# The first two feed-forward blocks of a decoder layer as products of 512 columns

## The chip, the core and the metric

The kernel runs on one core of a Trainium2 chip. The metric is the device time of one execution in microseconds (us); before the change three runs took 1160.81, 1161.96 and 1163.36 us, median 1161.96. One further execution was profiled. A core has a matrix engine (TensorE, PE in the profile; its weight loads are listed as PEld), a vector engine (VectorE, DVE), a scalar engine (ScalarE, ACT), GpSimd (POOL) and a queue that issues transfers (SyncE, SP). A product `lhsT.T @ rhs` on TensorE loads `lhsT` (128 x 128 here) as weights and then streams `rhs`; "a product of 512 columns" streams 512.

## The reference

Two decoder layers on 256 tokens of width 1024. Each has an input projection to 12800 columns that feeds a short convolution, an attention in three head groups and a spatial gating; their gated sum goes through `w_o` and a layer norm; then comes the part that the change touches:

```
h = silu(x @ w_gate) * (x @ w_up)          # w_gate, w_up: 1024 x 2816
x = layer_norm(ALPHA * x + h @ w_down)     # w_down: 2816 x 1024
```

## The kernel before

Everything is float32, and each product of two float32 matrices is done as three products of rounded parts: a matrix is split into a high part h (a rounded copy, made on ScalarE, L179) and a low part l (the rest, made on VectorE, L180), and the kernel sums h·h, h·l and l·h. Activations stay on the chip as such pairs: `xh`, `xl` hold x transposed (features on partitions, 256 tokens). Weights come from memory as panels of 1 MB (class `Panel`, L144), three of them in flight, and are split piece by piece: a piece is 128 partitions x 512 columns, four pieces to a panel, one ScalarE and one VectorE instruction each.

Two helpers issue the products. `feat` (L250) computes a result transposed, 256 features by 256 tokens: a 128 x 128 part of the weights is the stationary side, x streams with 256 columns, and it takes 48 products (L246 to L248) a panel. `toks` (L263) computes a result with tokens on partitions: 128 tokens of x are the stationary side and the weights stream (L266 to L268).

A layer is a list of steps in program order: spatial gating values, attention values, rotary keys and queries, convolution, gating, branch gates, `w_o` (with the norm of each tile of 128 tokens behind it), then the feed-forward blocks of 256 columns, numbered 0 to 10, then `w_down`. Blocks 2 to 10 go through `feat`, a step for the gate and one for the up part. Blocks 0 and 1 are in `ff_first` (L790) and go through `toks`, tile by tile, since tile 0 of x is normed and transposed before tile 1. Their result is in token order and has to be transposed back: `turn_h` (L808) does it on TensorE with the identity, and splits it into `hT`.

The order of instructions on each engine is written out by a pacing routine. Every product adds an estimated cost (`spend`), and each 1300 ns of it gives a `tick` (L209). A tick runs one entry of a list of hooks, among them the transposes of x (`to_features`, L296) and `turn_h`, and splits up to two more weight pieces, depending on how many are ahead of use and whether a hook is pending. So the place of a transpose among the products, and of a split among the work of ScalarE and VectorE, follows from these counts.

Of the kernel before, what the change touches and what calls it, by code (L numbers as in the profile page):

```python
# [14 lines left out]
AF = mybir.ActivationFunctionType  # L15
OP = mybir.AluOpType
# [79 lines left out]
def trunk(ctx: ExitStack, tc: tile.TileContext, a, out):  # L96
    nc = tc.nc
    V = nc.vector
# [11 lines left out]
    def flat(name, dt=F32):  # L110
        live[0] += 1
        assert live[0] <= NS, name
        return sl.tile([128, 512], dt, tag="slot", name=name)

    def slot(name, dt=F32):
        return flat(name, dt).rearrange("p (b s) -> p b s", b=2)

    def free(n=1):
        live[0] -= n
# [4 lines left out]
    def acc():  # L124
        return pa.tile([128, 512], F32, tag="acc", name="acc")

    def trp():
        return pt.tile([128, 512], F32, tag="trp", name="trp")

    con = cp.tile([128, C_N], F32, name="con")  # L130
    ident = con[:, C_ID:C_ID + 128]
# [45 lines left out]
    def split(h, l, src):  # L177

        nc.scalar.activation(h, src, AF.Copy)  # L179
        V.tensor_tensor(l, src, h.bitcast(F32), op=OP.subtract)  # L180
# [15 lines left out]
    def used(n=1):  # L196

        free(2 * n)

    hooks = deque()  # L200
# [8 lines left out]
    def tick():  # L209

        clock[1] += 1
        loaded = False
        while timed and timed[0][0] <= clock[1]:
            timed.pop(0)[1]()
            loaded = True
        if hooks:
            hooks.popleft()()
        clock[2] += PACE if slow else 0
        if clock[2] >= 1:
            clock[2] -= 1  # L220
            slow.popleft()()
            loaded = True
        lead = cnt["made"] - cnt["front"]
        if clock[1] <= cnt["calm"] and lead >= CALM:
            n = 0
        elif lead < LOW:
            n = 2
        elif loaded:
            n = 1 if lead < HIGH else 0
        elif slow:  # L230
            n = 2 if lead < TOP else 1
        else:
            n = 1 + (clock[1] % 2 and not hooks)
        for _ in range(n):
            if cnt["made"] != cnt["hold"] and cnt["split"] < len(panels) and live[0] + 2 + SPARE <= NS:
                piece()

    def spend(ns):
        clock[0] += ns
        if clock[0] >= TICK:  # L240
            clock[0] -= TICK
            tick()
# [7 lines left out]
    def feat(p, rhs):  # L250

        ps = acc()
        for b in range(2):
            for k in range(p.kc):
                mm3(ps[:, b * S:(b + 1) * S], p.at(k, b * 128, 128), *rhs(k), k == 0, k == p.kc - 1)
                if b == 1 and k % 2 == 1:
                    used()
                if b == 0 or k < p.kc - 1:
                    spend(327)
        spend(327)  # L260
        return ps.rearrange("p (b s) -> p b s", b=2)

    def toks(ps, lhs, p, k, c, n, first, last):  # L263

        h, l = p.at(k, c, n)
        nc.tensor.matmul(ps, lhsT=lhs[0], rhs=h, start=first, stop=False)  # L266
        nc.tensor.matmul(ps, lhsT=lhs[0], rhs=l, start=False, stop=False)  # L267
        nc.tensor.matmul(ps, lhsT=lhs[1], rhs=h, start=False, stop=last)  # L268
        if not last:
            spend(1.28 * n)  # L270
# [13 lines left out]
    def xtok(k, t):  # L284
        c = slice(t * 128, (t + 1) * 128)
        return xh[:, k, c], xl[:, k, c]
# [122 lines left out]
    def layer(L, steps):  # L409
# [7 lines left out]
        def half(w, kh, nh):  # L417
            return Panel(w[kh * 512:(kh + 1) * 512, nh * 512:(nh + 1) * 512], 4, 512)
# [89 lines left out]
        c = OFF_V  # L508
# [18 lines left out]
        for g in range(NG):  # L527
            c = OFF_ATT + (3 * g + 2) * GCOL
# [259 lines left out]
        hT = {}  # L788

        def ff_first(P):  # L790

            for j in range(2):
                hT[j] = (slot(f"hh{j}", F32R), slot(f"hl{j}", F32R))
            for t in range(2):
                for j in range(2):
                    ps = acc()
                    for w in range(2):
                        for k in range(8):
                            toks(ps[:, w * 256:(w + 1) * 256], xtok(k, t), P[2 * j + w], k, 0, 256, k == 0, k == 7)
                            if t and k % 2 == 1:  # L800
                                used()
                        if w == 0:
                            spend(328)
                    s = flat("hs")[:, :256]
                    nc.scalar.activation(s, ps[:, :256], AF.Silu)
                    V.tensor_tensor(s, s, ps[:, 256:], op=OP.mult)

                    def turn_h(s=s, t=t, j=j):  # L808
                        pp = trp()
                        for b in range(2):  # L810
                            nc.tensor.transpose(pp[:, b * 128:(b + 1) * 128], s[:, b * 128:(b + 1) * 128], ident)
                        c = (slice(None), slice(None), slice(t * 128, (t + 1) * 128))
                        split(hT[j][0][c], hT[j][1][c], pp[:, :256].rearrange("p (b s) -> p b s", b=2))
                        free()

                    hooks.extend([lambda: None] * 2 + [turn_h])
                    spend(328)

        def ff_gate(j):
            def f(P):  # L820
                ps = feat(P[0], xf)
                s = st["s"] = slot("hs")
                nc.scalar.activation(s, ps, AF.Silu)
            return f

        def ff_up(j):
            def f(P):
                ps = feat(P[0], xf)
                s = st["s"]
                V.tensor_tensor(s, s, ps, op=OP.mult)  # L830
                hT[j] = (slot(f"hh{j}", F32R), slot(f"hl{j}", F32R))
                split(hT[j][0], hT[j][1], s)
                free()
            return f

        ff = [Panel(a[w][L][:, j * 256:(j + 1) * 256], 8, 256) for j in range(11) for w in ("w_gate", "w_up")]
        steps.append((ff[:4], ff_first))
        for j in range(2, 11):
            steps.append(([ff[2 * j]], ff_gate(j)))
            steps.append(([ff[2 * j + 1]], ff_up(j)))  # L840

        dn = {}

# [43 lines left out]
    steps, starts = [], {}  # L887
    for L in range(DEPTH):
        n = len(steps)
        starts[n] = layer(L, steps)  # L890
# [59 lines left out]
```

## Time and profile before

| what | value |
|---|---|
| median of three runs | 1161.96 us |
| profiled execution | 1162.87 us, of which span 1160.8 us |
| PE busy | 1149.6 us (99% of the span) |
| DVE busy | 771.9 us (66%) |
| ACT busy | 619.0 us (53%) |
| granted TensorE clock, mean | 0.998 of full speed |

The busy time of PE says that a product was in flight nearly always, not how far apart products start. Matmuls overlap one another in the trace (a row of 0.28 us can be followed by the next 0.11 us later), so the pace is read from the starts of two rows and the number of products between them.

### The profile page before, as it was taken

What the parts mean: (1) busy time and instruction counts of PE and PEld (TensorE: products, weight loads), DVE (VectorE), ACT (ScalarE), POOL (GpSimd) and SP (SyncE); (2) the same over time, 40 slices, a digit from 0 to 9 for tenths busy, and PEclk for the clock granted to TensorE, in tenths of its full rate; (3) what the DMA queues carried; (4) which work ended last, traced back from release to release, by engine and by line L of the source; (5) the groups of instructions that cost most, each with busy time, mean ns of one, the idle gap of its engine ahead of it and who ended that gap; (6) DMA issues with size and microseconds to landing.
All of it is one profiled execution on the core that took longest, in us unless ns stands there. A gap on an engine that the chain in (4) does not pass through costs nothing.

```text
span 1160.8 us, 21675 instructions
## 1 busy us (share of the span) xinstructions
PE 1149.6 (99%) x8884; PEld 1093.9 (94%) x8884; DVE 771.9 (66%) x1394; ACT 619.0 (53%) x1144; POOL 14.1 (1%) x29
## 2 busy tenths in 40 slices
PE   9999999999999999999999999999999999999997
PEld 7899999999999999998888999999999999999985
DVE  6978778667556776546497677775765568754534
ACT  6655665665445365445175556666654445653530
POOL 0000000000000000000100000000000000000000
PEclk9999999999999999999999999999999999999999
DMA  9688545368557378448357564544666574764630
GB/s 339 211 259 239 169 154 183 112 200 280 165 183 233 105 251 272 162 146 304 131 190 259 171 189 137 182 150 142 211 225 198 175 245 134 253 195 147 215 112 36
DMA packets 180695, 222.41 MB, mean 192 GB/s; under 512 B 5456, under 2 KB 154228, under 8 KB 180596
## 3 DMA queue, kind: packets, MB, share of 16 engines
q1 hardware_dynamic: 178500, 214.66, 56.6%
q0 software_dynamic: 1952, 6.31, 1.7%
q8 instruction: 69, 1.13, 0.4%
q14 instruction: 30, 0.25, 0.1%
q10 hardware_dynamic: 144, 0.07, 0.0%
HBM read 213.67 MB, written 1.05 MB: 185 GB/s over the span
## 4 chain that ended last, share of the span: by engine, by line
PE 94%; DVE 2%; DMA 1%; ACT 1%; issue 1%; SPq 0%; DVEq 0%; ACTq 0%
PE acc L246 21%; PE acc L247 20%; PE acc L248 20%; PE acc L268 9%; PE acc L266 9%; PE acc L267 9%; PE acc L629 1%; PE trp L619 1%; DVE wl L180 1%; DMA raw<-in_w_in 1%; PE acc L708 1%; PE trp L296 1%; PE trp L599 0%; DMA xt<-in_x 0%; DMA sw<-qk 0%
## 5 line engine op out<-in xcount | busy, mean ns | idle before, releaser
L180 DVE TENSOR_TENSOR wl<-raw,wh 128x512 fp32r<-128x512 f32 x776 | 490.5, 686 | 194.7 <-ACT wh L179 188.4
L246 PE MATMUL acc<-xh,wh 128*128 128x256 f32 x1856 | 521.5, 281 | 0.0
L248 PE MATMUL acc<-xh,wl 128*128 128x256 f32 x1856 | 517.4, 279 | 0.4 <-DVE wl L180 0.4
L247 PE MATMUL acc<-xl,wh 128*128 128x256 f32 x1856 | 517.2, 279 | 0.0
L179 ACT ACTIVATE wh<-raw 128x512 fp32r<-128x512 f32 x776 | 429.5, 621 | 66.8 <-DMA raw<-in_w_in 28.3
L248 PEld LDWEIGHTS acc<-xh,wl 128*128 128x128 f32 x1856 | 351.2, 189 | 0.6 <-DVE wl L180 0.6
L246 PEld LDWEIGHTS acc<-xh,wh 128*128 128x128 f32 x1856 | 349.4, 188 | 2.5 <-issue 1.4
L247 PEld LDWEIGHTS acc<-xl,wh 128*128 128x128 f32 x1856 | 349.1, 188 | 0.1
L266 PE MATMUL acc<-wh,xh 128*128 128x512 f32 (+1 forms) x288 | 100.5, 349 | 0.2 <-ACT xh L179 0.2
L267 PE MATMUL acc<-wl,xh 128*128 128x512 f32 (+1 forms) x288 | 98.9, 344 | 0.3 <-DVE wl L180 0.3
L268 PE MATMUL acc<-wh,xl 128*128 128x512 f32 (+1 forms) x288 | 99.1, 344 | 0.0
L266 PE MATMUL acc<-wh,hh 128*128 128x512 f32 x176 | 68.7, 390 | 0.0
L268 PE MATMUL acc<-wh,hl 128*128 128x512 f32 x176 | 68.6, 390 | 0.0
L267 PE MATMUL acc<-wl,hh 128*128 128x512 f32 x176 | 68.6, 390 | 0.0
L267 PEld LDWEIGHTS acc<-wl,xh 128*128 128x128 f32 x288 | 54.9, 191 | 7.1 <-DVE wl L180 1.0
L266 PEld LDWEIGHTS acc<-wh,xh 128*128 128x128 f32 x288 | 54.8, 190 | 6.8 <-ACT xh L179 0.5
L268 PEld LDWEIGHTS acc<-wh,xl 128*128 128x128 f32 x288 | 54.9, 190 | 6.5 <-DVE xl L180 0.4
L179 ACT ACTIVATE hh<-hs 128x512 fp32r<-128x512 f32 x18 | 11.4, 632 | 61.8 <-DVE hs L830 61.8
L316 ACT ACTIVATE sd<-mv,eps 128x1 f32<-128x1 f32 x12 | 3.5, 295 | 74.2 <-DVE mv L313 74.1
L337 DVE SCALAR_TENSOR_TENSOR xt<-xt,acc 128x512 f32<-128x512 f32 x16 | 11.0, 687 | 45.7 <-PE acc L268 45.7
L268 PEld LDWEIGHTS acc<-wh,hl 128*128 128x128 f32 x176 | 33.0, 188 | 6.8
L267 PEld LDWEIGHTS acc<-wl,hh 128*128 128x128 f32 x176 | 33.1, 188 | 6.8
(148 smaller groups left out, 1261.9 us busy)
## 6 DMA issues: line engine op xcount, KB each, us to landing
raw<-in_w_in SPq DMA_DIRECT2D x99, 1024.0 KB, 5.2
raw<-in_w_gate SPq DMA_DIRECT2D x22, 1024.0 KB, 5.6
raw<-in_w_up SPq DMA_DIRECT2D x22, 1024.0 KB, 5.3
raw<-in_w_down SPq DMA_DIRECT2D x22, 1024.0 KB, 4.8
raw<-in_p_a SPq DMA_DIRECT2D x8, 1024.0 KB, 5.2
raw<-in_p_c SPq DMA_DIRECT2D x8, 1024.0 KB, 5.3
raw<-in_w_o SPq DMA_DIRECT2D x8, 1024.0 KB, 5.4
sw<-qk SPq DMA_DIRECT2D x96, 64.0 KB, 2.6
```

What stands on the lines that cost most here:

```text
L179: nc.scalar.activation(h, src, AF.Copy)
L180: V.tensor_tensor(l, src, h.bitcast(F32), op=OP.subtract)
L246: nc.tensor.matmul(o, lhsT=hl[0], rhs=rhs_h, start=first, stop=False)
L247: nc.tensor.matmul(o, lhsT=hl[0], rhs=rhs_l, start=False, stop=False)
L248: nc.tensor.matmul(o, lhsT=hl[1], rhs=rhs_h, start=False, stop=last)
L266: nc.tensor.matmul(ps, lhsT=lhs[0], rhs=h, start=first, stop=False)
L267: nc.tensor.matmul(ps, lhsT=lhs[0], rhs=l, start=False, stop=False)
L268: nc.tensor.matmul(ps, lhsT=lhs[1], rhs=h, start=False, stop=last)
L296: nc.tensor.transpose(ps[:, k * 128:(k + 1) * 128], xt[:, t, (4 * q + k) * 128:(4 * q + k + 1) * 128], ident)
L619: nc.tensor.transpose(ps[:, i * 128:(i + 1) * 128], p[:, i * 128:(i + 1) * 128], ident)
L629: nc.tensor.matmul(o[64 * r:64 * r + 64, t * 128:(t + 1) * 128], lhsT=va[g, kt][:, h * 64:(h + 1) * 64], rhs=state["t", b, t, r][:, i * 12 ...
L708: nc.tensor.matmul(sp[:, (2 * b + n) * 128:(2 * b + n + 1) * 128], lhsT=vv, rhs=st["wsT"][g // 4][:, g % 4, :], start=True, stop=True)
```

## The change

Blocks 0 and 1 are taken together. The weights of both come as half panels of 512 rows by 512 columns (as those of `w_o` do) in place of panels of 1024 rows by 256 columns, two for the gate and two for up. For each tile of 128 tokens the gate of both blocks is one chain of 24 products of 512 columns into one PSUM bank, and up is another into a second bank; before, each block had a bank, with gate and up in its halves, and 48 products of 256 columns. Silu and the multiplication run once a tile on 512 columns, and `turn_h` makes one visit of four transposes a tile where it made two visits of two; its two splits into `hT` stay of 256 columns. Bytes loaded, pieces split and columns streamed stay the same.

```diff
@@ -792,29 +792,29 @@
             for t in range(2):
-                for j in range(2):
-                    ps = acc()
-                    for w in range(2):
-                        for k in range(8):
-                            toks(ps[:, w * 256:(w + 1) * 256], xtok(k, t), P[2 * j + w], k, 0, 256, k == 0, k == 7)
-                            if t and k % 2 == 1:
-                                used()
-                        if w == 0:
-                            spend(328)
-                    s = flat("hs")[:, :256]
-                    nc.scalar.activation(s, ps[:, :256], AF.Silu)
-                    V.tensor_tensor(s, s, ps[:, 256:], op=OP.mult)
-
-                    def turn_h(s=s, t=t, j=j):
-                        pp = trp()
-                        for b in range(2):
-                            nc.tensor.transpose(pp[:, b * 128:(b + 1) * 128], s[:, b * 128:(b + 1) * 128], ident)
-                        c = (slice(None), slice(None), slice(t * 128, (t + 1) * 128))
-                        split(hT[j][0][c], hT[j][1][c], pp[:, :256].rearrange("p (b s) -> p b s", b=2))
-                        free()
-
-                    hooks.extend([lambda: None] * 2 + [turn_h])
-                    spend(328)
+                ps = [acc(), acc()]
+                for w in range(2):
+                    for k in range(8):
+                        toks(ps[w], xtok(k, t), P[2 * w + k // 4], k % 4, 0, 512, k == 0, k == 7)
+                        if t:
+                            used()
+                    if w == 0:
+                        spend(656)
+                s = flat("hs")
+                nc.scalar.activation(s, ps[0], AF.Silu)
+                V.tensor_tensor(s, s, ps[1], op=OP.mult)
+
+                def turn_h(s=s, t=t):
+                    pp = trp()
+                    for b in range(4):
+                        nc.tensor.transpose(pp[:, b * 128:(b + 1) * 128], s[:, b * 128:(b + 1) * 128], ident)
+                    c = (slice(None), slice(None), slice(t * 128, (t + 1) * 128))
+                    for j in range(2):
+                        split(hT[j][0][c], hT[j][1][c], pp[:, j * 256:(j + 1) * 256].rearrange("p (b s) -> p b s", b=2))
+                    free()
+
+                hooks.extend([lambda: None] * 2 + [turn_h])
+                spend(656)
...
-        ff = [Panel(a[w][L][:, j * 256:(j + 1) * 256], 8, 256) for j in range(11) for w in ("w_gate", "w_up")]
-        steps.append((ff[:4], ff_first))
+        ff = {(j, w): Panel(a[w][L][:, j * 256:(j + 1) * 256], 8, 256) for j in range(2, 11) for w in ("w_gate", "w_up")}
+        steps.append(([half(a[w][L], kh, 0) for w in ("w_gate", "w_up") for kh in range(2)], ff_first))
```

The last lines of the diff only fetch the panels of blocks 2 to 10 by name instead of by number.

In the program the change moves instructions at these places. On TensorE, the last visit of `turn_h` in layer 0 stands inside the gate product of block 2 (`acc` is a bank of sums, `trp` a bank for transposes, `hs` silu times up, `con` the identity, `wh` and `wl` the parts of a weight piece; the number behind a name tells one buffer from another). Before it had two transposes:

```order
L246 MATMUL acc_5362<-xh_77,wh_5161 128x256
L247 MATMUL acc_5362<-xl_78,wh_5161 128x256
L248 MATMUL acc_5362<-xh_77,wl_5162 128x256
L811 MATMUL trp_5398<-con_75,hs_5359 128x128 x2
L246 MATMUL acc_5362<-xh_77,wh_5161 128x256
L247 MATMUL acc_5362<-xl_78,wh_5161 128x256
L248 MATMUL acc_5362<-xh_77,wl_5162 128x256
L246 MATMUL acc_5362<-xh_77,wh_5165 128x256
```

The same place now:

```order
L246 MATMUL acc_5262<-xh_77,wh_5122 128x256
L247 MATMUL acc_5262<-xl_78,wh_5122 128x256
L248 MATMUL acc_5262<-xh_77,wl_5123 128x256
L810 MATMUL trp_5300<-con_75,hs_5259 128x128 x4
L246 MATMUL acc_5262<-xh_77,wh_5122 128x256
L247 MATMUL acc_5262<-xl_78,wh_5122 128x256
L248 MATMUL acc_5262<-xh_77,wl_5123 128x256
L246 MATMUL acc_5262<-xh_77,wh_5126 128x256
```

The visit has four transposes instead of two. In layer 0 it stands behind 27 products of `feat`, as before, and 837 follow without a break, as before. In layer 1 it stands behind 21 products where it stood behind 33, so 843 follow where 831 did.

On VectorE, from the end of the norm of tile 1 on, in layer 0 (lines with - are before, with + now; `xl` is the low part of the transposed x of tile 1, `hl` that of `hT`):

```order
 L327 SCALAR_TENSOR_TENSOR xt<-xt,sd,gb 128x512
-L180 TENSOR_TENSOR wl<-raw,wh 128x512 x3
-L806 TENSOR_TENSOR hs<-hs,acc 128x256
-L180 TENSOR_TENSOR wl<-raw,wh 128x512
+L180 TENSOR_TENSOR wl<-raw,wh 128x512 x4
 L180 TENSOR_TENSOR xl<-trp,xh 128x4x128
 L180 TENSOR_TENSOR wl<-raw,wh 128x512 x2
 L180 TENSOR_TENSOR xl<-trp,xh 128x4x128
 L180 TENSOR_TENSOR wl<-raw,wh 128x512 x4
-L806 TENSOR_TENSOR hs<-hs,acc 128x256
-L180 TENSOR_TENSOR wl<-raw,wh 128x512
+L805 TENSOR_TENSOR hs<-hs,acc 128x512
```

The first multiplication of silu and up no longer stands among the weight pieces of tile 0; the one of 512 columns stands behind all of them. Ten pieces of the 16 that tile 0 needs are split ahead of the norm, before as now. On TensorE the transposes of tile 1 of x stand behind 33 and 39 products of 512 columns in layer 0 (30 and 36 in layer 1), where they stood behind 66 and 75 of 256 (57 and 69).

## Rows read from the trace of the kernel before

**Rows 1.** The page's first part: busy us (share of the span) xinstructions.
```profile
PE 1149.6 (99%) x8884; PEld 1093.9 (94%) x8884; DVE 771.9 (66%) x1394; ACT 619.0 (53%) x1144; POOL 14.1 (1%) x29
```
**Rows 2.** Timeline of PE: start us, duration us, line, operation; far-apart products of `feat`.
```profile
278.92 0.28 PE L248 MATMUL acc<-xh,wl 128*128 128x256 f32 x1
...
294.90 0.28 PE L248 MATMUL acc<-xh,wl 128*128 128x256 f32 x1
...
425.04 0.28 PE L247 MATMUL acc<-xl,wh 128*128 128x256 f32 x1
...
514.90 0.28 PE L248 MATMUL acc<-xh,wl 128*128 128x256 f32 x1
```
**Rows 3.** PE in the stretch 1000 to 1090 us: busy (products), clock, DMA share, GB/s.
```profile
1000.00:1090.00 90.00, 90.00 (x766) 1.00 0.60 198
```
**Rows 4.** Timeline of PE at the last visit of `turn_h`, layers 0 and 1.
```profile
418.09 0.28 PE L246 MATMUL acc<-xh,wh 128*128 128x256 f32 x1
...
420.70 0.28 PE L248 MATMUL acc<-xh,wl 128*128 128x256 f32 x1
420.81 0.38 PE L811 MATMUL trp<-con,hs 128*128 128x128 f32 x2
...
421.15 0.28 PE L247 MATMUL acc<-xl,wh 128*128 128x256 f32 x1
...
994.03 0.38 PE L811 MATMUL trp<-con,hs 128*128 128x128 f32 x2
```
**Rows 5.** Timeline of PE at two visits of four transposes (L442) between `feat` products.
```profile
65.19 0.28 PE L248 MATMUL acc<-xh,wl 128*128 128x256 f32 x1
...
67.31 0.28 PE L248 MATMUL acc<-xh,wl 128*128 128x256 f32 x1
67.43 0.60 PE L442 MATMUL trp<-con,ws 128*128 128x128 f32 x4
...
67.99 0.28 PE L247 MATMUL acc<-xl,wh 128*128 128x256 f32 x1
68.11 0.28 PE L248 MATMUL acc<-xh,wl 128*128 128x256 f32 x1
...
73.21 0.28 PE L248 MATMUL acc<-xh,wl 128*128 128x256 f32 x1
73.33 0.60 PE L442 MATMUL trp<-con,ws 128*128 128x128 f32 x4
...
73.88 0.28 PE L247 MATMUL acc<-xl,wh 128*128 128x256 f32 x1
...
79.10 0.28 PE L248 MATMUL acc<-xh,wl 128*128 128x256 f32 x1
```
**Rows 6.** Timeline of PE at a visit of eight transposes (L619) in attention.
```profile
163.50 1.03 PE L619 MATMUL trp<-con,p 128*128 128x128 f32 x8
...
164.61 0.28 PE L248 MATMUL acc<-xh,wl 128*128 128x256 f32 x1
...
168.50 0.28 PE L248 MATMUL acc<-xh,wl 128*128 128x256 f32 x1
```
**Rows 7.** Timeline of PE, products of `toks`: `w_o`, `ff_first`, and layer 1's gating values.
```profile
371.30 0.39 PE L268 MATMUL acc<-wh,ml 128*128 128x512 f32 x1
...
389.00 0.40 PE L268 MATMUL acc<-wh,ml 128*128 128x512 f32 x1
...
393.80 0.28 PE L268 MATMUL acc<-wh,xl 128*128 128x256 f32 x1
...
401.22 0.28 PE L268 MATMUL acc<-wh,xl 128*128 128x256 f32 x1
...
592.12 0.39 PE L268 MATMUL acc<-wh,xl 128*128 128x512 f32 x1
...
608.00 0.40 PE L268 MATMUL acc<-wh,xl 128*128 128x512 f32 x1
```
**Rows 8.** Timeline of VectorE: first weight pieces behind the norm of tile 1, layer 0.
```profile
399.50 1.89 DVE L180 TENSOR_TENSOR wl<-raw,wh 128x512 fp32r<-128x512 f32 x3
```

More of the change, by code (lines that the diff above doesn't have):

```diff
@@ L834, in ff_up @@
             return f
-        ff = [Panel(a[w][L][:, j * 256:(j + 1) * 256], 8, 256) for j in range(11) for w in ("w_gate", "w_up")]
-        steps.append((ff[:4], ff_first))
+        ff = {(j, w): Panel(a[w][L][:, j * 256:(j + 1) * 256], 8, 256) for j in range(2, 11) for w in ("w_gate", "w_up")}
+        steps.append(([half(a[w][L], kh, 0) for w in ("w_gate", "w_up") for kh in range(2)], ff_first))
         for j in range(2, 11):
-            steps.append(([ff[2 * j]], ff_gate(j)))
-            steps.append(([ff[2 * j + 1]], ff_up(j)))
+            steps.append(([ff[j, "w_gate"]], ff_gate(j)))
+            steps.append(([ff[j, "w_up"]], ff_up(j)))
         dn = {}
```

## The prediction

> **What bounds the kernel now.** I read the page's engine shares first: PE is busy for 1149.6 of 1160.8 us [rows 1], so nothing that the other engines save counts by itself; what counts is how far apart products start. That is read from the timeline of PE, by two far rows of a stretch and the number of products from one to the other. The same kind of product, `feat` with 256 columns of x, turns out to run at two paces. From 278.92 to 294.90 us 142 products start [rows 2]: 15.98 us over 141 steps, 113.3 ns each. From 425.04 to 514.90 us, in the feed-forward blocks, 764 start [rows 2]: 89.86 over 763 steps, 117.8 ns each. The stretch from 1000 to 1090 us in layer 1 holds 766 products, a clock of 1.00 and a DMA share of 0.60 [rows 3]; two of the 766 began ahead of it, so 90/764, again 117.8 ns. Both paces come at the full granted clock, and a stretch keeps its pace through hundreds of products, over many weight panels and banks. I call them the close and the wide pace, by the distance of the products.
>
> Where does a pace change? The place that this change touches shows it. In layer 0 the feed-forward blocks from number 2 on begin at the close pace: 24 products from 418.09 to 420.70 [rows 4], 2.61 over 23 steps, 113.5 ns. Then comes the last `turn_h`, two transposes at 420.81 [rows 4], and behind it all 837 remaining products of the stretch are at the wide pace; in layer 1 the visit at 994.03 [rows 4] does the same, and 831 wide ones follow. So the visit decides between the two paces until the next interruption. What differs inside I can't see; I take it as how a product and the weight load beside it lie against each other.
>
> **The change part by part.**
>
> *Products of 512 columns.* A layer loses 192 products of 256 columns and gains 96 of 512. Before: 64 products from 393.80 to 401.22 [rows 7], 7.42/63 = 117.8 ns, so 192 x 117.8 = 22.62 us. The new kind, x as weights and 512 columns streaming, stands in layer 1's gating values: 70 products from 592.12 to 608.00 [rows 7], 15.88/69 = 230.1 ns, so 96 x 230.1 = 22.09 us. Gain 0.53 us a layer, 1.06 in both. From below, `w_o` with its 79 products from 371.30 to 389.00 [rows 7] has 17.70/78 = 226.9 ns, which would give 0.84 a layer, 1.68 in all; from above, two of the old products take 235.6 ns, a gain of nothing. I take 230.1, since there too x is the stationary side.
>
> The Trainium skill, "TensorE: Matmul & The Clock Gate", section "Back-to-back issue gap", gives N/2.4 + 2.5 ns for an isolated product at the full clock: an estimate by it is 2.5 ns saved for each pair, 0.24 us a layer. The rows here stand 9 to 14 ns above that formula, so it gives half of the term above.
>
> *The visits of* `turn_h`. A visit of two: from 420.70 to 421.15 [rows 4] is 0.45 us where two close steps take 0.227, so 0.22 us. A visit of four: from 67.31 to 67.99 [rows 5] is 0.68 where two wide steps take 0.236, so 0.44 us. Eight visits of two cost 1.8 us, four of four 1.8 us: nothing changes.
>
> *The pace behind the last visit.* This is the large term, and the trace has no visit of four at just this place. Its nearest rows are two visits of four transposes (L442) with the same operands, the identity streaming and a 512-column slot as weights. The first interrupts a wide stretch (19 products from 65.19 to 67.31, 2.12/18 = 117.8 ns) that follows on products of `toks` with 512 columns; behind it 46 products from 68.11 to 73.21 take 5.10/45 = 113.3 ns. The second, at 73.33, interrupts that close stretch, and behind it 47 products from 73.88 to 79.10 take 5.22/46 = 113.5 ns [rows 5]. So both visits of four were followed by the close pace, whichever pace they met. The changed kernel copies the first case closely: `feat` follows on 512-column products, and in layer 1 the visit stands behind 21 products, as the one at 67.43 does. So I take the close pace: 837 + 831 = 1668 products at 4.45 ns less are 7.42 us. Against it, `feat` now follows on 512-column products and may begin wide, as at 65.19: 27 + 21 products ahead of the visit at 4.45 ns more, 0.21 us. The term is 7.2 us; its other end is zero (both layers at the wide pace as now, where I also take the 0.21 as lost, 0.2 us below nothing).
>
> *Hidden parts.* Silu and the multiplication run once on 512 columns instead of twice on 256; VectorE and ScalarE are busy 66% and 53% [rows 1], and nothing on PE needs `hT` until `w_down`. The cover that matters is the weight supply of tile 0: it needs 16 pieces within 48 products, ten of them split ahead of the norm. VectorE starts the next three at 399.50 and takes 1.89 us for them [rows 8], the first done at about 400.1. Tile 0 begins two steps of 0.118 ahead of 393.80 [rows 7], at 393.57. The eleventh piece is wanted behind 30 products, at 393.57 + 30 x 0.230 = 400.5, its low part one product later, 400.7. The margin is some 0.6 us, where it was about as much; behind it the change takes one multiplication out of the row of pieces. The transposes of tile 1 of x come at 393.57 + 33 x 0.230 = 401.2, behind the norm that ended when VectorE turned to pieces at 399.50 [rows 8]. If this cover goes, PE waits by what VectorE is late, some tenths of a us. The new panels have rows of 2 KB for 1 KB in the same 1 MB; no load is waited for there, so nothing is booked.
>
> *Sum.* 1.06 + 0 + 7.2 = 8.3 us. The profiled execution took 1162.87 us (span 1160.8 and 2.1 around), which gives 1154.6; the median of the runs is 0.9 lower, 1161.96, so 1153.7 us.
>
> **The rivals.**
>
> *A, the forecast.* Both last visits, of four now, are followed by the close pace: 1153.7, with 1153.0 if 512-column products run as in `w_o`, and 1154.8 if they gain nothing. About 0.7 either way for what a median of three leaves open: 1152.3 to 1155.4.
>
> *B, one layer only.* The two layers reach their visit behind 27 and 21 products, so they can end in different paces: 1161.96 - 1.06 - 3.6 = 1157.3.
>
> *C, the wide pace stays.* The change then does what it says and little comes of it: 1161.96 - 1.06 + 0.2 = 1161.1, at the best 1160.3. For it: a visit is no sure switch. One of eight transposes at 163.50 is followed by 34 products from 164.61 to 168.50 at 3.89/33 = 117.9 ns [rows 6]; and both visits at the very place of the change end wide. Against it: of the 18 visits of four or eight transposes in a row with 256-column `feat` products behind them 16 are followed by the close pace, and the other two have eight.
>
> The Trainium skill, "TensorE: Matmul & The Clock Gate", section "Step-by-step: what each phase is for", says that loading the next weights takes no SBUF read bandwidth from the running product, as each has its own port. By that rule how loads and products lie should not matter, and a visit could not set a pace; the time would be that of C. The rows with two paces at one clock speak against it, so C keeps its chance from the exceptions alone.
>
> *D, slower.* Weight pieces of tile 0 come late. Place: VectorE behind the norm of tile 1, with the low parts of x, 0.7 us each as the pieces' 0.63, in among the last pieces. If a transpose of x slips by more than the 0.6 us of margin, what stands behind it (two pieces, then the other low part) is late, and PE waits up to about 1.9 us a layer. It decides only if the wide pace stays too: 1161.1 + 3.8 = 1164.9. No wait of PE there in the trace now, and one instruction fewer in that row on VectorE, speak against it.
>
> **How the numbers follow.** A 0.60, B 0.10, C 0.25, D 0.05. The prediction is A's 1153.7 us. The range takes in A and B (0.70) and the half of C that lies lower, up to 1161.2: 1152.3 to 1161.2. About 0.2%, 2.3 us, is what a measurement can tell from no change. Faster by more, below 1159.6, are A, B and a little of C: 0.72. Within it is nearly all of C: 0.23. Slower is D: 0.05.
>
> **What would show it.** In the profile of the changed kernel, the starts of `feat` products from the last `turn_h` on: some 794 in a stretch of 90 us if close, 764 if wide, in each layer by itself. The first 27 and 21 products ahead of the visit show whether `feat` begins wide. 96 products of 512 columns should take 22.1 us a layer less their visits. A visit of four should cost 0.44 us. A gap ahead of a product in tile 0 that ends on VectorE would show D. If both stretches are wide, the large term is wrong and what is left is 1 us.

## The result, and the profile after

The changed kernel takes 1155.73 us (median of nine runs, 1153.4 to 1159.5 but for one of 1259 in which the granted clock was 0.85 of full speed), the kernel before 1161.7: a ratio of 0.9945, 95% interval 0.9932 to 0.9957. The forecast was 1153.7 with a range of 1152.3 to 1161.2. The execution that was profiled took 1159.47 us, the longest of the other eight. Its page, first part (busy us, share of the span, instructions):

```profile
span 1157.6 us, 21279 instructions
## 1 busy us (share of the span) xinstructions
PE 1146.5 (99%) x8692; PEld 1081.8 (93%) x8692; DVE 771.9 (67%) x1390; ACT 619.5 (54%) x1140; POOL 14.2 (1%) x29
```

PE is still in use for 99% of the span [rows 1], so the pace of its products is again what to read. PE in three stretches: the feed-forward blocks of layer 0, the rotary products of layer 1 and the feed-forward blocks of layer 1 (columns: the stretch, its length, busy time and the number of products, clock, DMA share, GB/s):

```profile
425.00:505.00 80.00, 80.00 (x709) 1.00 0.64 211
646.00:686.00 40.00, 40.00 (x342) 1.00 0.61 183
1000.00:1075.00 75.00, 75.00 (x639) 1.00 0.57 187
```

The same stretches of the kernel before:

```profile
425.00:505.00 80.00, 80.00 (x681) 1.00 0.67 221
646.00:686.00 40.00, 40.00 (x342) 1.00 0.61 179
1000.00:1075.00 75.00, 75.00 (x639) 1.00 0.61 200
```

A count is the whole finding: 709 products in 80 us is the close pace (113.3 ns, with the two or three that began ahead of the stretch), 681 the wide one (117.8 ns). Layer 0 has changed from wide to close, layer 1 has not. The clock is at its full level in all six rows.

Where the time went is read from the starts of products at the borders of stages, here of the kernel after (first product of `ff_first`, of block 2 and of `w_down`, in layers 0 and 1):

```profile
394.92 0.39 PE L266 MATMUL acc<-wh,xh 128*128 128x512 f32 x1
...
418.39 0.28 PE L246 MATMUL acc<-xh,wh 128*128 128x256 f32 x1
...
516.78 0.39 PE L266 MATMUL acc<-wh,hh 128*128 128x512 f32 x1
...
963.25 0.39 PE L266 MATMUL acc<-wh,xh 128*128 128x512 f32 x1
...
986.71 0.28 PE L246 MATMUL acc<-xh,wh 128*128 128x256 f32 x1
...
1088.85 0.39 PE L266 MATMUL acc<-wh,hh 128*128 128x512 f32 x1
```

| stage | before, us | after, us | difference |
|---|---|---|---|
| up to `ff_first`, layer 0 | 393.57 | 394.92 | +1.35 |
| `ff_first`, layer 0 | 24.17 | 23.47 | -0.70 |
| blocks 2 to 10, layer 0 | 101.88 | 98.39 | -3.49 |
| from there to `ff_first`, layer 1 | 446.48 | 446.47 | 0.0 |
| `ff_first`, layer 1 | 24.17 | 23.46 | -0.71 |
| blocks 2 to 10, layer 1 | 101.85 | 102.14 | +0.29 |
| from there to the end of the span | 68.7 | 68.7 | 0.0 |

The first row is no effect of the change: the two programs are the same there, and in this execution the first loads came later (the first product of `toks` starts at 8.13 us, at 6.86 before); a second trace of the same changed kernel has 393.93 there. Without it the execution would lie near 1158.1 us, by rival B, one layer only, 1157.3. But the median run is over 2 us faster than that, which one trace can't explain. So the experiments ask two things: what sets the pace behind the last visit, and is it the same in each execution?

### The profile page after: what moved, and what is told of

It is laid out like the page before. It is cut to its first block, busy times and chain, and to the rows that moved or that the text cites. A ratio compares the mean times of both kernels' runs of the same rounds, so it can differ in the third digit from the quotient of the medians.

```text
span 1157.6 us, 21279 instructions
## 1 busy us (share of the span) xinstructions
PE 1146.5 (99%) x8692; PEld 1081.8 (93%) x8692; DVE 771.9 (67%) x1390; ACT 619.5 (54%) x1140; POOL 14.2 (1%) x29
## 4 chain that ended last, share of the span: by engine, by line
PE 93%; DVE 3%; DMA 1%; ACT 1%; issue 1%; SPq 0%; DVEq 0%; ACTq 0%
PE acc L246 20%; PE acc L248 20%; PE acc L247 20%; PE acc L266 9%; PE acc L267 9%; PE acc L268 9%; PE acc L629 1%; PE trp L619 1%; DVE wl L180 1%; PE acc L708 1%; DMA raw<-in_w_in 1%; PE trp L296 1%; PE trp L599 0%; DMA xt<-in_x 0%; DMA sw<-qk 0%
## 5 line engine op out<-in xcount | busy, mean ns | idle before, releaser
L266 PE MATMUL acc<-wh,xh 128*128 128x512 f32 x224 | 89.9, 401 | 0.3 <-ACT xh L179 0.3
L267 PE MATMUL acc<-wl,xh 128*128 128x512 f32 x224 | 88.6, 396 | 0.0
L268 PE MATMUL acc<-wh,xl 128*128 128x512 f32 x224 | 88.5, 395 | 0.0
L266 PE MATMUL acc<-wh,hh 128*128 128x512 f32 x176 | 68.7, 390 | 0.0
L266 PEld LDWEIGHTS acc<-wh,xh 128*128 128x128 f32 x224 | 43.1, 192 | 9.3 <-ACT xh L179 0.5
L268 PEld LDWEIGHTS acc<-wh,xl 128*128 128x128 f32 x224 | 42.9, 192 | 9.4 <-DVE xl L180 0.4
L267 PEld LDWEIGHTS acc<-wl,xh 128*128 128x128 f32 x224 | 43.1, 192 | 8.7 <-DVE wl L180 0.2
L266 PEld LDWEIGHTS acc<-wh,hh 128*128 128x128 f32 x176 | 33.0, 188 | 6.8
```

## The experiments

Each verdict is a ratio to the kernel before in the same series, whose medians lay between 1161.7 and 1163.1 us; the single executions stand beside one of it of 1164.27.

**The changed kernel again** (no edit), and later a third time.

> The changed kernel once more, unaltered. Its first profile shows the close pace (113.3 ns) behind the last visit in layer 0 and the wide one (117.8 ns) in layer 1, at 1159.5 us, while eight of its runs lie between 1153.4 and 1159.5. Theory V (the pace behind the visit hangs on how the visit happens to fall, anew in each execution): this profile may show another mix, and its time follows it, about 3.7 us for each of the two stretches; median again near 1155.7. Rival F (each layer's pace is fixed by the program, the spread has another source): again close in layer 0 and wide in layer 1, whatever the time.

Measured: 1155.38 us, ratio 0.9942 (0.9920 to 0.9963). Its profiled execution took 1158.47 us and again had layer 0 close and layer 1 wide.

> The changed kernel once more, for a third trace. Two traces had layer 0 close and layer 1 wide behind the last visit, at 1159.5 and 1158.5 us, while other executions took 1153.4 to 1156.8. If the program fixes the pace (F), layer 1 is wide again; if each execution draws it (V), it may be close, and then the time should be about 1154.5.

Measured: 1155.87 us, and PE of this execution reads

```profile
425.00:505.00 80.00, 80.00 (x708) 1.00 0.65 211
646.00:686.00 40.00, 40.00 (x342) 1.00 0.61 181
1000.00:1075.00 75.00, 75.00 (x664) 1.00 0.60 197
```

664 products in the third stretch in place of 639: layer 1 is close here. One program, two paces at one place in different executions. This run was on another chip than the second one, but the chip doesn't settle it: the two scans below ran on the chip of this run, with the same program up to the last visit of layer 0, and behind that visit layer 0 is wide in the first scan and close in the second. So layer 0 is no sure thing either, close in four of five such traces. F has fallen. The three profiled executions took 1159.5 and 1158.5 us with one layer close and 1155.9 with both, and the runs without a trace between 1153.4 and 1158.3; that most of these had both close is argued from their times, as they have no trace.

**The old products with visits of four.**

```diff
             for t in range(2):
+                both = []
                 for j in range(2):
...
+                    both.append(s)
...
-                        for b in range(2):
-                            nc.tensor.transpose(pp[:, b * 128:(b + 1) * 128], s[:, b * 128:(b + 1) * 128], ident)
+                    for b in range(4):
+                        nc.tensor.transpose(pp[:, b * 128:(b + 1) * 128], both[b // 2][:, b % 2 * 128:(b % 2 + 1) * 128], ident)
```

> The kernel before with its products of 256 columns, but with the two transposes of block 0 and the two of block 1 of a tile in one visit of four (the last one behind 27 and 33 products of block 2, as before, with 837 and 831 behind it). Theory V: the visit alone brings the large part of the gain: at least one of the two stretches at 113.3 ns, 3.7 us for each, so 1154.5 to 1158 us against 1161.7. Rival W (the pace comes from what stands ahead of it, the 512-column products or the half panels): both stretches stay at 117.8 ns, 1161.7 us.

Measured: 1156.06 us, ratio 0.9944 (0.9930 to 0.9959), and

```profile
425.00:505.00 80.00, 80.00 (x708) 1.00 0.65 211
...
1000.00:1075.00 75.00, 75.00 (x664) 1.00 0.62 200
```

Both stretches are close without a single product of 512 columns in these blocks. Grouping the transposes alone brings nearly all of the gain; W has fallen.

**The new products with visits of two.**

```diff
-                    for b in range(4):
-                        nc.tensor.transpose(pp[:, b * 128:(b + 1) * 128], s[:, b * 128:(b + 1) * 128], ident)
+                    for b in range(2):
+                        nc.tensor.transpose(pp[:, b * 128:(b + 1) * 128], s[:, (2 * j + b) * 128:(2 * j + b + 1) * 128], ident)
...
-                hooks.extend([lambda: None] * 2 + [turn_h])
+                hooks.extend([lambda: None] * 2 + [lambda f=turn_h: f(0), lambda f=turn_h: f(1)])
```

> The changed kernel with its 512-column products, but its visits of four taken apart again into two visits of two, one tick (12 products) apart; the last has 825 and 831 products behind it. Theory V: behind visits of two both stretches are at 117.8 ns as in the kernel before; what is left is the products' term, 0.5 us a layer: about 1160.7 us. Rival W: the stretches are at 113.3 ns as far as they were with visits of four, and the time is that of the changed kernel, about 1155.7 us.

Measured: 1155.29 us, ratio 0.9938 (0.9924 to 0.9953). Not what V said: both stretches are close, and the time is the one that W gave, though W can't account for the run before this one.

```profile
425.00:505.00 80.00, 80.00 (x708) 1.00 0.65 211
...
1000.00:1075.00 75.00, 75.00 (x664) 1.00 0.60 197
```

In layer 1 the trace shows the close pace up to the first visit of two (its transposes start at 988.84), the wide one for the 12 products behind it, and the close one behind the second, at 990.47. In layer 0 both visits met the wide pace, and the first left it wide, the second close. So it isn't that two transposes leave the wide pace; what a visit leaves depends on more than its length.

**The last visit out of the way.**

```diff
-                hooks.extend([lambda: None] * 2 + [turn_h])
+                if t == 0:
+                    hooks.extend([lambda: None] * 2 + [turn_h])
+                else:
+                    st["turn"] = turn_h
...
         def ff_up(j):
             def f(P):
+                if j == 10:
+                    st["turn"]()
```

> The changed kernel with the last visit of each layer moved from behind 27 and 21 products to the middle of the last block (816 products ahead of it, 48 behind). Theory V: nothing interrupts the 816 products, so they keep the pace with which they begin behind the 512-column products; where that is close, as in both layers of the changed kernel's first profile, both stretches run at 113.3 ns and the time is about 1153.5 us; where it is wide, 1161. A rival by which layer 1's feed-forward stage is bound to the wide pace by its place (other loads, other buffers) has layer 1 at 117.8 ns again, 1157 us or more.

Measured: 1155.03 us, ratio 0.9931 (0.9914 to 0.9948); 816 products close in both layers (708 and 664 in the two stretches). Nothing in the stage itself forces the wide pace. (The late visit met the close pace in both layers and left the 48 products behind it wide in layer 0, close in layer 1.)

**Which visits leave which pace.** Sixteen visits a layer that do nothing but interrupt, ahead of each panel's first product; `visits` holds eight times 1 and eight times 2 in layer 0, eight times 3 and eight times 4 in layer 1.

```diff
-    def feat(p, rhs):
+    def feat(p, rhs, at=None, n=0):
...
             for k in range(p.kc):
+                if b * p.kc + k == at:
+                    pp = trp()
+                    for i in range(n):
+                        nc.tensor.transpose(pp[:, i * 128:(i + 1) * 128], xt[:, 0, i * 128:(i + 1) * 128], ident)
```

> The changed kernel with 16 further visits in each layer's blocks 3 to 10, each of transposes of x that nobody reads, ahead of a panel's first product: in layer 0 eight visits of one transpose, then eight of two; in layer 1 eight of three, then eight of four. Each is followed by 48 products, whose starts tell the pace. From the runs so far: two transposes met the close pace three times and left the wide one each time; they met the wide one three times and left it wide once and close twice. Theory P (a visit shifts how products and weight loads lie against each other by its length, and the pace that it leaves follows from its length and the pace it meets): for each number of transposes the same pace met leads to the same pace left nearly always; two turn close into wide and come back at the next or the one after it. Rival R (each visit draws the pace afresh): for each number both paces follow without order. Time: 160 transposes at 0.11 us more, and half the blocks at either pace.

Measured: 1165.11 us in one execution (the edit adds 80 transposes, not the 160 of the expectation). Timeline of PE, the second transpose of each of the eight visits of two in layer 0 (start us, duration, line, operation):

```profile
475.45 0.27 PE L258 MATMUL trp<-con,xt 128*128 128x128 f32 x1
...
481.33 0.27 PE L258 MATMUL trp<-con,xt 128*128 128x128 f32 x1
...
487.02 0.27 PE L258 MATMUL trp<-con,xt 128*128 128x128 f32 x1
...
492.71 0.27 PE L258 MATMUL trp<-con,xt 128*128 128x128 f32 x1
...
498.59 0.27 PE L258 MATMUL trp<-con,xt 128*128 128x128 f32 x1
...
504.28 0.27 PE L258 MATMUL trp<-con,xt 128*128 128x128 f32 x1
...
509.97 0.27 PE L258 MATMUL trp<-con,xt 128*128 128x128 f32 x1
...
515.85 0.27 PE L258 MATMUL trp<-con,xt 128*128 128x128 f32 x1
```

From one visit to the next, each time 48 products and two transposes: 5.88, 5.69, 5.69, 5.88, 5.69, 5.69, 5.88 us. Wide, close, close, wide, close, close, wide: an order of three, no draw.

> As the run before it, with each visit behind the panel's first 21 products instead of ahead of them. Theory P: the place doesn't matter, the same pace met and number of transposes lead to the same pace left. A rival by which the place in the panel (which part of x and of the weights is read around the visit) decides has other sequences here.

Measured: 1167.1 us. With the visits at another place in the panel the order of three is the same: behind the visits of two come close, close, wide, close, close, wide, close, close. Taking both runs, 16 visits for each number:

| transposes in the visit | close pace behind it |
|---|---|
| 1 | 3 of 16 |
| 2 | 11 of 16 |
| 3 | 15 of 16 |
| 4 | 15 of 16 |

Of the visits of three and of four it is only the first of a row that missed. The pace that a visit leaves is ordered by its length, but the pace that it meets isn't all that counts: of two visits of two that meet the close pace one goes on close and the next turns wide. It looks like a hidden position, which a visit of two moves through three places, and which differs from execution to execution where a row begins.

**One more visit in the old kernel.** The kernel before, with four transposes added that nobody reads.

```diff
         def ff_up(j):
             def f(P):
+                if j == 2:
+                    pp = trp()
+                    for i in range(4):
+                        nc.tensor.transpose(pp[:, i * 128:(i + 1) * 128], xt[:, 0, i * 128:(i + 1) * 128], ident)
```

> The kernel before, unaltered but for one further visit of four transposes of x that nobody reads, ahead of block 2's up panel in each layer (21 and 15 products behind the last turn_h, 816 ahead of the next break). It adds 0.44 us of work a layer and removes none. In all traces so far a visit of four that met the wide pace left the close one, 9 of 9. Theory P: both stretches run at 113.3 ns, 2 x 816 x 4.45 ns = 7.3 us less, 0.9 us more for the visits, so 6.4 us faster than the kernel before without it (about 1155.5 to 1156.5 by the runs so far). Rival N (the paces are a by-product of other things in the stage, such as when loads or splits fall): 0.9 us slower than before.

Measured: 1157.49 us, ratio 0.9953 (0.9941 to 0.9966). Timeline of PE around the added visit in layer 0, and PE in the two stretches:

```profile
424.59 0.28 PE L248 MATMUL acc<-xh,wl 128*128 128x256 f32 x1
424.71 0.60 PE L831 MATMUL trp<-con,xt 128*128 128x128 f32 x4
425.06 0.37 PE L246 MATMUL acc<-xh,wh 128*128 128x256 f32 x1
```

```profile
425.00:505.00 80.00, 80.00 (x708) 1.00 0.69 224
1000.00:1075.00 75.00, 75.00 (x664) 1.00 0.62 201
```

With eight instructions more and none less the kernel is 5.3 us faster: 681 and 639 products have become 708 and 664. This is the plainest proof that the pace, and no work that the change saves, is the large term. It gained 1.1 us less than the 6.4 expected. The trace shows where: blocks 2 to 10 take 98.70 and 98.67 us in the two layers for 101.88 and 101.85, which is 6.36 us less, as expected, but the stage up to `ff_first` of layer 0, which the edit doesn't touch, takes 394.77 us for 393.57.

**Both visits side by side, meant to make sure of it.**

```diff
+            visits = []
...
-                hooks.extend([lambda: None] * 2 + [turn_h])
+                visits.append(turn_h)
+                if t:
+                    hooks.extend([lambda: None] * 2 + visits)
```

> The changed kernel with tile 0's visit of four held back to stand in block 2's gate and up products too, 12 products behind that of tile 1's place in the order, so that two visits of four follow each other there and no work is added. Theory P: where the first leaves the wide pace the second turns it close, so both layers are close in every execution: median about 1154.3, and none of the executions near 1158 that the changed kernel has (its fast executions lay between 1153.4 and 1159.5). Rival: the spread of the changed kernel has nothing to do with layer 1's pace and is the same here.

Measured: 1162.2 us, ratio 0.9992 (0.9982 to 1.0001): no gain is left that can be told from nothing. A miss, and the most useful one.

```profile
425.00:505.00 80.00, 80.00 (x682) 1.00 0.63 206
1000.00:1075.00 75.00, 75.00 (x639) 1.00 0.60 195
```

Both layers are wide behind the second visit, in this kernel and in the next, four stretches of four. Visits of four 48 products apart kept the close pace in all but the first of a row; 12 products apart they end in the wide one. The products of 512 columns are all there and still save 1.2 us by the stages of this trace, but the large term is gone. Four stretches in two executions are no rule: two of the twelve runs of this kernel, of 1158.97 and 1159.57 us, are some 3 us faster than its median. One close layer is worth 3.7 us, so they may be such cases; they have no trace.

**The rotary products too.** As before, and the transposes of layer 1's spatial weights are held back into the stretch of rotary products, which was wide in all but one trace.

```diff
+            if not first:
+                hooks.extend([lambda: None] * 22)
             for f in st["later"]:
                 hooks.extend([lambda: None] * 3 + [f])
```

> As the run before it, and in layer 1 the two visits of four that transpose the spatial weights (and the one of the filter taps) are held back by 22 ticks, from the attention values into the rotary products, whose 456 products run at the wide pace in eight of nine traces. Theory P: from the second of these visits on some 400 products run at 113.3 instead of 117.8 ns, 1.7 to 2.0 us less than the run before it, about 1152.5. A rival: holding hooks back slows the splitting of weight pieces and PE waits for pieces, no gain or a loss.

Measured: 1160.01 us, ratio 0.9980 (0.9971 to 0.9989), 2.2 us below the run before it, which shares the wide feed-forward stretches. The rotary stretch now holds

```profile
646.00:686.00 40.00, 40.00 (x353) 1.00 0.70 210
```

353 products for 342. A second place, with the same cause and the expected size.

**All of it together, with either width.** Last visit late (as in the fourth experiment) and rotary products, in the changed kernel and in the kernel before.

> The changed kernel with its last visit of each layer in the last block, behind 816 products, and with layer 1's spatial visits held back into the rotary products. Theory P: 816 products in each layer keep the close pace with which they begin behind the 512-column products, and some 430 of the rotary products turn close (2.2 us in the pair of runs that has shown it): 1155.0 - 2.0 = 1153.0 us, about 9.7 us under the kernel before. Against it: the pace at the start is drawn too, and where it comes out wide in one layer the time is 1156.6.

Measured: 1152.79 us, ratio 0.9913 (0.9900 to 0.9927), with all three stretches close:

```profile
425.00:505.00 80.00, 80.00 (x708) 1.00 0.62 203
646.00:686.00 40.00, 40.00 (x353) 1.00 0.72 217
1000.00:1075.00 75.00, 75.00 (x664) 1.00 0.55 183
```

This is the fastest version, 2.9 us below the changed kernel's median; that one is of another series, and by the two ratios it is 3.7 us.

> The kernel before, with its products of 256 columns and visits of two, and with the same two moves. Theory P: the 256-column products were followed by the close pace in both layers of every trace, so both stretches and the rotary products are close: 7.2 us for the stretches and 2 us for the rotary products under the kernel before, about 1153.5; the distance to the run before this one is the term of the 512-column products, forecast as 1.06 us and 0.8 to 1.0 by the runs so far. Rival (the width of the products is worth more than that): over 2 us between the two.

Measured: 1154.59 us, ratio 0.9926 (0.9914 to 0.9939), the three stretches close as well. The two medians differ by 1.8 us. By the stages of the two traces `ff_first` is 0.71 us a layer shorter in the first, 1.42 in both, and blocks 2 to 10 are equal (98.4 us a layer): the late visit has four transposes for two, 0.22 more, and the last 48 products are close in the first and wide in the second, 0.21 less. The rest lies outside the stages that were changed. Of the 0.71 in `ff_first` 0.09 are the visits (below), so the width of the products is worth some 1.2 us by this pair.

## Why the prediction was right, and where not

*Products of 512 columns*, forecast 0.53 us a layer. From the first product of `ff_first` on 33 such products start without a break, up to

```profile
402.25 0.39 PE L268 MATMUL acc<-wh,xl 128*128 128x512 f32 x1
```

which is 402.25 - 394.92 = 7.33 us over 32 steps, 229.1 ns each. So 96 take 21.99 us for 22.62 before: 0.63 a layer, somewhat more than forecast. The mean of 230.1 from layer 1's gating values [rows 7] mixed two paces, 229 and, in its last quarter, 233 ns; the 226.9 of `w_o` would have been too kind.

*The visits*, forecast at no change. The first visit of four now stands among products of 512 columns:

```profile
410.02 0.40 PE L268 MATMUL acc<-wh,xl 128*128 128x512 f32 x1
410.32 0.66 PE L810 MATMUL trp<-con,hs 128*128 128x128 f32 x4
410.74 0.48 PE L266 MATMUL acc<-wh,xh 128*128 128x512 f32 x1
411.05 0.40 PE L267 MATMUL acc<-wl,xh 128*128 128x512 f32 x1
```

From 410.02 to 411.05 are 1.03 us where two steps take 0.46, so it costs 0.57 us, not 0.44. Three visits of two stood in `ff_first` before (0.66), so 0.09 are gained there; with the 0.63 of the products that is the 0.70 and 0.71 by which `ff_first` became shorter, to 0.02. In block 2 the visit of four for one of two costs more: blocks 2 to 10 of layer 0 gained 3.49 us where 837 products at 4.45 ns less are 3.72, and the difference, 0.23, is two transposes more. So the visits lose 0.14 us a layer, and with the 0.63 the two terms together come to 0.49 for 0.53 forecast: two small errors of opposite sign.

*The pace behind the last visit*, forecast 7.2 us. This was the right mechanism, and a place where the forecast was too sure. Of the three traced executions layer 0 was close in all, layer 1 in one. So the first trace is B's case and the third A's, and the median of the runs, 1155.7, lies just above the 1155.4 up to which A reached; the range held because it took in both. The forecast said that the changed kernel copies the visit at 67.43 [rows 5], in which four transposes met the wide pace. The step that failed is the pace met: `feat` turned close within its first five steps behind the 512-column products (in layer 0's stretch of 27 ahead of the visit as in layer 1's of 21), so the 0.21 us were not lost, and the copy was of the other case, a visit of four that meets the close pace. That one also stood in the rows, once, at 73.33, and it is no sure thing. The 16 of 18 that I counted against C were real, but the scans show an order where I had taken chances, so such a count gives no chance for one place.

The Trainium skill, "TensorE: Matmul & The Clock Gate", section "Step-by-step: what each phase is for", says that loading the next weights takes no SBUF read bandwidth from the running product; C drew from it that a visit could set no pace. That conclusion does not hold in these traces: 639 and 664 products of one kind in 75 us, at one clock, set apart by four transposes that nobody reads. Whether a load takes bandwidth from a product no run here shows.

*D, late weight pieces*, did not come: no product of `ff_first` waits for a piece in the trace after, and VectorE ran its pieces in the order that was reckoned. There is one small wait in its place, in each layer, that the prediction had put at nothing: the first visit of four waits for the multiplication of silu and up, which is now one of 512 columns.

```profile
410.32 0.42 PEld L810 LDWEIGHTS trp<-con,hs 128*128 128x128 f32 x4 [0.34 <-DVE hs L805]
```

Of these 0.34 us of the weight loads the row of products lost some 0.07 (0.30 from 410.02 to 410.32, where a step is 0.23); they are part of the 0.57 above.

*The sum.* 8.3 us were forecast; the medians differ by 6.0, and by 7.2 in the series of the second run. The third trace, with both layers close, has the same borders of stages at

```profile
395.10 0.39 PE L266 MATMUL acc<-wh,xh 128*128 128x512 f32 x1
...
418.56 0.28 PE L246 MATMUL acc<-xh,wh 128*128 128x256 f32 x1
...
516.95 0.39 PE L266 MATMUL acc<-wh,hh 128*128 128x512 f32 x1
...
963.40 0.39 PE L266 MATMUL acc<-wh,xh 128*128 128x512 f32 x1
...
986.86 0.28 PE L246 MATMUL acc<-xh,wh 128*128 128x256 f32 x1
...
1085.27 0.39 PE L266 MATMUL acc<-wh,hh 128*128 128x512 f32 x1
```

Its `ff_first` and blocks 2 to 10 are 0.71, 3.49, 0.71 and 3.44 us shorter than before, 8.35 in all: where both layers are close the forecast of the changed stages is right. The execution still took 1155.87 us and not the 1154.6 that was forecast for a profiled one, since `ff_first` of layer 0 begins 1.53 us later than in the one trace of the kernel before. Over all the traces that beginning lies between 393.5 and 395.1 us, though the programs are alike up to there, and why was not followed; the forecast was worked out from an early one. How much of what the median lacks comes from this and how much from executions with a wide layer can't be told, as the runs behind it have no trace.

What stays open is what the hidden position is. It seems to move by thirds under visits of two, it differs between executions, and 12 products between two visits act otherwise than 48. Nor is the pace there at once: in the third trace the four steps from 989.82 to 990.30 us, behind the last visit of layer 1, still take 0.12 us each before the close pace sets in. That products and weight loads lie in one of a few positions against each other fits all of this, but no view of the profile shows it, so it is argued, not shown.

## What to carry to other kernels

Where TensorE is busy all the time, the time is the number of products times the distance of their starts: take that distance for each stretch before pricing any edit, since a busy share of 99% hid two paces 4% apart here. If a long stretch runs at the wider one, look at the last short thing that interrupted it; in the kernel before, moving that interruption to the end of the stretch (1154.6 us, together with the rotary products) or grouping it otherwise (1156.1 us) was worth more than the wider products. And trace more than one execution: a gain that hangs on such a position can be there in one and not in the next, and a neighbouring edit can take it back (1162.2 us).

## What the runs showed of the hardware

- Products of 128 x 128 weights with 256 columns of x start 113.3 or 117.8 ns apart at the full granted clock. But for the first few behind a visit they keep to one of the two, for up to 843 in a row, whatever panel or bank.
- What streams counts too, with no interruption at all: in the branch gates of the kernel before 120 products that stream the branch results start 119.8 ns apart (264.29 to 278.55 us), and the 144 with x behind them 113.5 (278.67 to 294.90); it is so at every such turn in both layers.
- In two traces, interruptions by two transposes, 48 products apart, gave close, close, wide in a fixed order; those of three or four were at the close pace from the second on at the latest; single ones left the wide pace 13 times of 16.
- Two visits of four only 12 products apart left the wide pace four times of four, in two traces.
- With 512 columns and x as weights a product took 229.1 ns in `ff_first`, where two of 256 columns took 235.6 (twice 117.8, in every trace of such products). At the close pace, seen only where x streams, two would take 226.6: by that estimate the wider product gains only where the narrow ones run at the wide pace.
